# A hybrid decoder layer: all matmul tiles at one offset within 2 KB, an eleventh home for expert pieces

## The chip, the core and the metric

The kernel runs on one core of a Trainium2 chip. The metric is device time in microseconds (us), from the launch of the program on the core to its end; less is better. The engines have short names in the profile: PE (TensorE, matmuls), PEld (its loads of stationary operands), DVE (VectorE), ACT (ScalarE), POOL (GpSimd) and SP (SyncE, which here only issues transfers).

## What is computed

One decoder layer on 256 tokens of width 2048, in float32. Cut to what matters:

```python
h = rms_norm(x, attn_norm_g)
u, q, k, v, gate_ssm, gate_att = split(h @ w_in)          # w_in: 2048 x 8192
y_ssm = s5_mixer(u, ...)                                   # scan over 256 steps, gelu, z * sigmoid(z @ w_glu)
y_att = stick_breaking_attention(rms(q), rms(k), v)        # 8 heads of 128
merged = sigmoid(gate_ssm) * (y_ssm @ w_branch_ssm) + sigmoid(gate_att) * (y_att @ w_branch_att)
x = x + merged @ w_out
t = rms_norm(x, ffn_norm_g)
# router: best of 4 groups, best 2 of its 8 experts; 32 experts in all
for e in range(32):
    out += combine[:, e] * ((silu(t @ w_gate[e]) * (t @ w_up[e])) @ w_down[e])
x = x + out
```

The weights of one expert are 2048 x 1024 (gate and up) and 512 x 2048 (down) in float32, 12.6 MB; those of all experts are 403 MB.

## The kernel before

**Projections.** The weights of w_in, w_branch_att, w_glu, w_branch_ssm and w_out stream through the core in 200 *subs* of 512 KB: two slices of 128 rows by 512 columns each. For each sub, `dma` loads `raw`, and `split` makes two float32r tiles of it: `wh` (ACT, rounded) and `wl` (DVE, what the rounding left). `mm` of `b_orient` then runs twelve matmuls of 512 columns: `wh` against the activations' `xh` and `xl`, and `wl` against `xh`, for two slices and two halves of the tokens. `wh` and `wl` are the moving operand here, and a 128x128 slice of the activations is the stationary one. The names of the activations change with the block: `xh`, `xl` for w_in, `ya` for w_branch_att, `ys` for w_branch_ssm, `m` (`m0`, `m1`) for w_out. Only w_glu (`a_orient`) is the other way round: `wh` and `wl` are stationary, and `zz` is moving, with 256 columns.

The order is written out in a loop over the subs `i`. At each step it splits sub `i + 2`, loads sub `i + 5`, runs the matmuls of sub `i`, and lets the other work (statistics, scan of the state-space mixer, attention heads) take its turns by a rough count of each engine's load. The subs 0 to 143 are w_in and w_branch_att, 144 to 151 w_glu, 152 to 167 w_branch_ssm, 168 to 199 w_out. Three tiles each of `raw`, `wh` and `wl` go round.

**Homes.** Ten tiles of 16 KB a partition, one to a pool, hold large activations during the projections (`U[0]` to `U[9]`, without 6) and then, all but `U[0]` and `U[5]`, serve as homes for *pieces* of expert weights: 2 MB each, six to an expert, 192 in all. `ring` names the order: 8, 9, 2, 7, 4, 3, 1, and three more pools (`w0` to `w2`) where the projections' small tiles had been. `load_piece` takes the next piece and its home. The first six pieces are loaded in quarters of 512 KB from step 148 of the loop on, one quarter at every second step, behind four loads of `x2`; a seventh is loaded whole near the last step. A home can be loaded as soon as its earlier user is done. All these loads, and those of `raw`, stand in one queue on SP, in program order, so a load that waits holds up those behind it.

**Experts.** For each expert, 32 gathered tokens go through `gate_up` (XY stationary, the piece `ew` moving) and `down`; each piece that has been used frees its home for the next. Home 3 is given up after its second piece, since the result `accv` takes its place.

**Places.** The allocator lays the pools out in order, from byte 0 of each partition: 16 KB of scratch for the descriptors of transfers that POOL issues, 128 bytes of constants, the ten tiles of 16 KB, the small tiles (`cp`, `cq`), and then `wp` with `raw`, `wh` and `wl`, and `hp` with eight tiles of 2 KB (`ya` among them). So all the tiles of the first kind start at 128 within 2 KB, and `raw`, `wh`, `wl` and `ya` at 1824:

| tiles | used as | bytes from a partition's start | within 2 KB |
|---|---|---|---|
| xh, xl, m0, m1, ys | stationary | 16,512 to 131,199 | 128 |
| zz (w_glu) | moving | 147,584 | 128 |
| wh, wl | moving (stationary in w_glu) | 186,144 to 210,719 | 1824 |
| ya | stationary | 210,720 to 227,103 | 1824 |

A slice of `wh` or `wl` (512 floats) is 2 KB, and the stationary slices lie at multiples of 512 bytes from their tile's start.

Of the kernel before, what the change touches and what calls it, by code (L numbers as in the profile page):

```python
# [9 lines left out]
F32 = mybir.dt.float32  # L10
# [7 lines left out]
P = 128  # L18
# [18 lines left out]
X2_AT = 24  # L37
# [5 lines left out]


class Meter:
    """Forwards to an engine and adds up a rough length of what is emitted on it."""

    def __init__(self, eng, load, key):
        self.eng, self.load, self.key = eng, load, key
# [33 lines left out]
def hybrid_block(ctx, tc, A, out):  # L83
    nc = tc.nc
# [3 lines left out]
    pe = Meter(nc.tensor, load, "pe")  # L88
    sp, pool = nc.sync, nc.gpsimd

    U = {i: ctx.enter_context(tc.tile_pool(name=f"u{i}", bufs=1)) for i in range(10) if i != 6}

    def unit(i, shape, dt, name):
        return U[i].tile(shape, dt, name=name, tag="u")

# [5 lines left out]
    cq = wctx.enter_context(tc.tile_pool(name="cq", bufs=1))  # L101
# [9 lines left out]
    def bg_tile(k):  # L111
        return pbg.tile([P, 512], F32, name="bg" + "ab"[k], tag="bg" + "ab"[k])

    # ---------------------------------------------------------------- weight stream
    blocks = []

    def add_block(src, nk, begin, mm, fin):
# [6 lines left out]
    def dma(i):  # L124
        if i >= len(subs):
            return
        src, s = subs[i][:2]
        raw_t[i] = wp.tile([P, 2, 512], F32, name="raw", tag="raw")
        sp.dma_start(raw_t[i], src[:, 2 * s:2 * s + 2, :])

    def split(i):
        if i >= len(subs):
            return
        raw = raw_t.pop(i)
        h = wp.tile([P, 2, 512], F32R, name="wh", tag="wh")
        l = wp.tile([P, 2, 512], F32R, name="wl", tag="wl")
        act.copy(h, raw)
        vec.tensor_tensor(l, raw, h, op=OP.subtract)
        hl_t[i] = (h, l)

    # ---------------------------------------------------------------- first loads
    xh = unit(0, [P, 16, T], F32R, "xh")
    xl = unit(1, [P, 16, T], F32R, "xl")
    xT = unit(4, [P, 16, T], F32, "xT")
    g1 = cq.tile([P, 16], F32, name="g1")
    # projection blocks are declared below; the stream is started once they are known
    small = cq.tile([P, 3, 32], F32, name="lamdt")
    dsk = cq.tile([P, 16], F32, name="dsk")
    qkg = cq.tile([P, 2], F32, name="qkg")
    g2 = cp.tile([P, 16], F32, name="g2")  # L150
# [2 lines left out]

    ident = cp.tile([P, P], F32, name="ident")
    make_identity(nc, ident)
    pool.dma_start(small, A["lamdt"])
    ones = cp.tile([P, P], F32, name="ones")
    pool.memset(ones, 1.0)
    uge = cq.tile([P, P], F32, name="uge")
# [36 lines left out]
        vec.tensor_scalar(t, t, -0.5, 1.5, op0=OP.mult, op1=OP.add)  # L196
        vec.tensor_tensor(y, y, t, op=OP.mult)

    # ---------------------------------------------------------------- blocks of the projections
    rstd = cq.tile([P, 2], F32, name="rstd")  # L200
    rstdp = cq.tile([P, 2], F32, name="rstdp")
    uy = unit(2, [P, 2, 8, T], F32, "uy")
# [209 lines left out]
        for s in range(nk // 2):  # L412
            subs.append((src, s, nk, begin, mm, fin))

    # ---------------------------------------------------------------- start of the stream
    def x_prep(k0):
        for k in range(k0, k0 + 2):
            act.activation(xh[:, k], xT[:, k], AF.Copy, scale=g1[:, k:k + 1])
            vec.scalar_tensor_tensor(xl[:, k], xT[:, k], g1[:, k:k + 1], xh[:, k], op0=OP.mult, op1=OP.subtract)
# [61 lines left out]
        vec.tensor_scalar(qkg[:, 0:1], qkg[:, 0:1], float(P) ** -0.5, None, op0=OP.mult)  # L481
        yield 0.8

    # ---------------------------------------------------------------- state-space mixer
    coef = [cq.tile([P, 2, 2, 16], F32, name=f"coef{h}") for h in range(2)]
    prod = [cq.tile([P, 2, 2, 16], F32, name=f"prod{h}") for h in range(2)]

# [249 lines left out]
            yield 0  # L737
        prog["z"] = True

    # ---------------------------------------------------------------- stick-breaking attention  # L740
    hst = cq.tile([P, 3, 2, 2, 8], F32, name="hst")

    def attention():
# [80 lines left out]
        if len(YA) == 8:  # L824
            prog["att"] = True

    # ---------------------------------------------------------------- expert weight stream
    ring = [U[i] for i in (8, 9, 2, 7, 4, 3, 1)]
    used = [0]
    held = {}  # L830
    ahead = []
# [4 lines left out]
    nextp = [0]  # L836

    def load_piece():
        n = nextp[0]
        if n >= len(pieces):  # L840
            return
        j = n % 10 if n < 20 else (n - 20) % 9
        j += n >= 20 and j > 4
        if used[0] <= held.get(j, -1):
            return
        held[j] = n
        e, i = pieces[n]
        tl = ring[j].tile([P, 4, 1024], F32, name="ew", tag="u")
        src = A["wgu"][e][:, 4 * i:4 * i + 4] if i < 4 else A["wd"][e][:, 4 * i - 16:4 * i - 12]
        if n < 6:  # L850
            for k in range(4):
                ahead.append(lambda k=k: sp.dma_start(tl[:, k], src[:, k]))
        else:
            for c0, cw in (((0, 1024),) if n < len(pieces) - 1 else ((0, LSPLIT), (LSPLIT, 1024 - LSPLIT))):
                sp.dma_start(tl[:, :, c0:c0 + cw], src[:, :, c0:c0 + cw])
        ptile[e, i] = tl
        nextp[0] += 1

    # ---------------------------------------------------------------- main stream
    gens = [init_stats(), attention(), ssm()]  # L860
    next(gens[2])
    pend = []
# [25 lines left out]
    first_out = nsub - 32  # L888
    for i in range(nsub):
        prog["step"] = i  # L890
        src, s, nk, begin, mm, fin = subs[i]
        if i < 6:
            x_prep(2 * i + 4)
        split(i + 2)
        dma(i + 5)
        if s == 0:
            begin()
        h, l = hl_t.pop(i)
        mm(s, h, l)
        run_pend()  # L900
        if s == nk // 2 - 1:
            fin()
        pe0 = load["pe"]
        for g in (gens[:1] if i < HOLD else list(gens)):
            while rest.get(g, 0) <= i:
                if load["pe"] > pe0 + BURST or load["vec"] > load["pe"] + SLACK or load["act"] > load["pe"] + SLACK:
                    break
                c = next(g, None)
                if c is None:
                    gens.remove(g)  # L910
                    break
                if c <= 0:
                    rest[g] = i + 1 - c
        load["vec"] = max(load["vec"], load["pe"] - CREDIT)
        load["act"] = max(load["act"], load["pe"] - CREDIT)
        if i == first_out - X2_AT:
            S["x2"] = unit(5, [P, 2, D], F32, "x2")
            for t in range(2):
                for c in range(2):
                    cs = slice(1024 * c, 1024 * c + 1024)  # L920
                    ahead.append(lambda t=t, cs=cs: sp.dma_start(S["x2"][:, t, cs], A["x"][t][:, cs]))
        if i >= first_out - X2_AT and (i % 2 == 0 or i < first_out - X2_AT + 4):
            if not ahead and nextp[0] < 6:
                load_piece()
            if ahead:
                ahead.pop(0)()
        if i == nsub - 4:
            load_piece()
# [6 lines left out]
    for i in range(3):  # L935
        ring.append(ctx.enter_context(tc.tile_pool(name=f"w{i}", bufs=1, reuse_waits="tile")))

    # ---------------------------------------------------------------- router
    def keep_busy(n):
        ps = acc_tile()  # L940
        for _ in range(n):
# [36 lines left out]
    m1, m2 = R4[:, 2], R4[:, 3]  # L978
# [26 lines left out]
    Go = R32[:, 5].rearrange("p t g e -> p t (g e)")  # L1005

    def gates():
        # gate of the first choice: 1 / ((1 + exp(m2 - m1)) * sum of the group softmax)
        vec.tensor_scalar(w1, dif, 1.0, None, op0=OP.add)
        vec.tensor_tensor(w1, w1, gsum[:, :, None].to_broadcast([P, 2, 4]), op=OP.mult)  # L1010
        vec.reciprocal(w1, w1)
        vec.tensor_tensor(w2_, w1, dif, op=OP.mult)
        vec.tensor_tensor(oh1, oh1, w1[:, :, :, None].to_broadcast([P, 2, 4, 8]), op=OP.mult)
        vec.tensor_tensor(oh2, oh2, w2_[:, :, :, None].to_broadcast([P, 2, 4, 8]), op=OP.mult)
        vec.tensor_tensor(R32[:, 2], oh1, oh2, op=OP.add)
        vec.scalar_tensor_tensor(Go, rank, float(CAP), G, op0=OP.is_ge, op1=OP.mult)

    def overflow():
        # experts with more tokens than slots, as a list of ids behind its length
        ps = bg_tile(1)  # L1020
        for t in range(2):
            pe.matmul(ps[0:32, 0:1], M[:, t], ones[:, 0:1], start=(t == 0), stop=(t == 1))
        vec.tensor_scalar(OV[:, 0:1], ps[0:32, 0:1], float(CAP), None, op0=OP.is_gt)
        vec.tensor_tensor(OV[:, 33:34], OV[:, 0:1], eidx[0:32], op=OP.mult)
        pe.matmul(ps[0:32, 1:2], ult[0:32, 0:32], OV[:, 0:1], start=True, stop=True)
        vec.tensor_copy(OV[:, 34:35], ps[0:32, 1:2])
        vec.tensor_scalar(OV[:, 1:33], iota[0:32], OV[:, 34:35], OV[:, 33:34], op0=OP.is_equal, op1=OP.mult)
        pe.matmul(ps[0:1, 2:35], ones[0:32, 0:1], OV[:, 0:33], start=True, stop=True)
        vec.tensor_copy(oli, ps[0:1, 2:35])
# [2 lines left out]
    XB = XY[:, 0]  # L1032
    Y4 = XY[:, 1].rearrange("p a b -> p (a b)")

    # ---------------------------------------------------------------- experts
    SC = [None, None]

    def gather(q):
# [91 lines left out]
            if q == NE // 4 - 1:  # L1130
                sp.dma_start(out[t][:, c], accv[:, t, c])

    while nextp[0] < 10:
        load_piece()
    for e in range(NE - 2):
        hT = gate_up(e, gather(e // 4) if e % 4 == 0 else iter(()))
# [20 lines left out]
    scatter(q, 2, (1,))  # L1157
    scatter(q, 3)

    # ---------------------------------------------------------------- tokens beyond the slots  # L1160
    accv = S["acc"]
    XO = unit(2, [P, 16, T], F32, "XO")
    WO = [unit(u, [P, 4, 1024], F32, f"WO{u}") for u in (4, 9, 7, 0)]
# [3 lines left out]
    with tc.For_i(0, novr) as it:  # L1167
        er = nc.values_load(oli[0:1, bass.ds(it + 1, 1)], min_val=0, max_val=NE - 1)
        gp = [acc_tile() for _ in range(4)]
        for k4 in range(4):  # L1170
# [8 lines left out]
            for i in range(4):  # L1179
                k = 4 * k4 + i  # L1180
                for t in range(2):
                    for hf in range(2):
                        pe.matmul(gp[2 * t + hf], XO[:, k, P * t:P * t + P], WO[k4][:, i, 512 * hf:512 * hf + 512],
                                  start=(k == 0), stop=(k == 15))
# [12 lines left out]
        for t in range(2):  # L1197
            for n in range(4):
                ps = acc_tile()
                for j in range(4):  # L1200
                    pe.matmul(ps, hOT[:, j, P * t:P * t + P], WO[n // 2][:, j, 512 * (n % 2):512 * (n % 2) + 512],
                              start=(j == 0), stop=(j == 3))
# [57 lines left out]
```

## Time and profile before

| what | value |
|---|---|
| three runs | 1598.7, 1601.5 and 1602.9 us |
| median | 1601.51 us |
| profiled execution | span of 1600.2 us, from the first to the last instruction |
| PE busy | 1284.2 us (80%), mean granted clock 0.924 |
| DVE, ACT, POOL busy | 522.9, 451.0 and 43.7 us |
| moved by DMA | 519 MB, 324 GB/s over the span |

The profile is of one execution. A slice or a stretch shows for each engine how long it was busy in it; PEclk is the granted clock of TensorE, 1.00 being 2.4 GHz; the DMA share is the mean busy share of the 16 DMA engines. Matmuls overlap, so the length of one record is more than the distance between two starts; the distance is what a stream of them costs. In the order of time, neighbouring instructions of one form are merged, with their count behind x.

### The profile page before, as it was taken

How to read it: one execution, taken by the hardware profiler on the slowest of the kernel's cores; microseconds unless marked ns; L12 is line 12 of the kernel's file. 1: busy time of each engine (PE TensorE's matmuls, PEld its weight loads, DVE VectorE, ACT ScalarE, POOL GpSimd, SP SyncE). 2: the span in 40 equal slices, each digit the busy share in tenths (PEclk: the TensorE clock that was granted, in tenths of full speed). 3: DMA queues.
4: the chain of work that ended last, by engine and by line, in shares of the span. 5: the costliest groups of instructions: out<-in, count | busy, mean ns of one | idle time of the engine just before them, and what ended most of it. 6: DMA issues, size and time to landing. Idle time of an engine off the chain costs nothing. (4 is left out here: it accounts for less than half of the span.)

```text
span 1600.2 us, 25136 instructions
## 1 busy us (share of the span) xinstructions
PE 1284.2 (80%) x10654; PEld 862.1 (54%) x10654; DVE 522.9 (33%) x1342; ACT 451.0 (28%) x769; POOL 43.7 (3%) x113
## 2 busy tenths in 40 slices
PE   8899999999999999986756656766656656756696
PEld 7777888888867888842423422423323323323364
DVE  5664877787745754410101101101001001001001
ACT  5455567544434443321111011011111111110101
POOL 8200000000000000000000000000000000000000
PEclk9999999999999999997988978978979978888999
DMA  7554645566644777799999999999999999999995
GB/s 270 174 159 147 195 147 157 159 189 193 186 143 160 261 263 261 297 411 429 427 426 428 425 430 425 428 427 427 428 427 428 426 427 428 427 428 426 427 426 233
DMA packets 64131, 519.01 MB, mean 324 GB/s; under 512 B 7680, under 2 KB 7680, under 8 KB 40208
## 3 DMA queue, kind: packets, MB, share of 16 engines
q1 hardware_dynamic: 63408, 515.22, 81.6%
q10 hardware_dynamic: 576, 2.10, 0.4%
q8 instruction: 86, 1.41, 0.4%
q14 instruction: 29, 0.24, 0.0%
q0 software_dynamic: 32, 0.05, 0.0%
HBM read 515.24 MB, written 2.10 MB: 323 GB/s over the span
## 5 line engine op out<-in xcount | busy, mean ns | idle before, releaser
L77 PE MATMUL acc<-ew,XY 128*32 128x256 f32 x4096 | 303.4, 448 | 170.0 <-DMA ew<-wgu 170.0
L77 PEld LDWEIGHTS acc<-ew,XY 128*32 128x32 f32 x4096 | 140.3, 124 | 317.2 <-DMA ew<-wgu 185.8
L77 DVE TENSOR_TENSOR wl<-raw,wh 128x1024 fp32r<-128x1024 f32 x200 | 244.3, 1225 | 173.3 <-ACT wh L77 168.3
L77 ACT CAST wh<-raw 128x1024 fp32r<-128x1024 f32 x200 | 209.0, 1051 | 198.1 <-PE acc L77 109.6
L77 DVE TENSOR_TENSOR sg<-sg,acc 128x128 f32<-128x128 f32 x32 | 9.2, 288 | 652.4 <-ACT sg L77 652.4
L77 PE MATMUL acc<-ew,hT 128*32 128x256 f32 (+1 forms) x2080 | 152.9, 445 | 76.2 <-DMA ew<-wd 46.1
L77 ACT COPY XY<-acc 32x256 f32<-32x256 f32 (+1 forms) x260 | 93.7, 360 | 220.1 <-PE acc L77 217.6
L77 PEld LDWEIGHTS acc<-ew,hT 128*32 128x32 f32 x2080 | 75.1, 125 | 143.8 <-issue 65.3
L77 PE MATMUL acc<-wh,xh 128*128 128x512 f32 x512 | 147.9, 406 | 3.4 <-ACT wh L77 3.4
L77 PE MATMUL acc<-wl,xh 128*128 128x512 f32 x512 | 144.0, 398 | 1.0 <-DVE wl L77 0.8
L77 PE MATMUL acc<-wh,xl 128*128 128x512 f32 x512 | 144.0, 398 | 0.0
L77 ACT ACTIVATE sg<-acc 128x128 f32<-128x128 f32 x32 | 8.9, 278 | 410.4 <-PE acc L77 410.4
L77 PEld LDWEIGHTS acc<-wl,xh 128*128 128x128 f32 x512 | 97.2, 190 | 25.6 <-DVE wl L77 2.7
L77 PEld LDWEIGHTS acc<-wh,xl 128*128 128x128 f32 x512 | 97.4, 190 | 23.1
L77 PEld LDWEIGHTS acc<-wh,xh 128*128 128x128 f32 x512 | 94.0, 191 | 25.6 <-ACT wh L77 5.6
L77 PE MATMUL acc<-XY,sc 128*128 128x512 f32 x128 | 63.9, 641 | 14.6 <-ACT XY L77 14.5
L77 PE MATMUL bga<-SL,x 128*128 128x128 f32 x512 | 63.5, 280 | 10.3 <-DVE SL L77 10.3
L77 PEld LDWEIGHTS bga<-SL,x 128*128 128x128 f32 x512 | 59.0, 192 | 22.9 <-DVE SL L77 15.9
L77 DVE TENSOR_TENSOR Vs<-Vs,prod 128x32 f32<-128x32 f32 x508 | 68.1, 189 | 0.0
L77 DVE TENSOR_TENSOR accv<-accv,acc 128x512 f32<-128x512 f32 x56 | 38.5, 688 | 86.5 <-PE acc L77 86.5
L77 PE MATMUL acc<-wh,m 128*128 128x512 f32 x256 | 66.4, 399 | 0.0
L77 PEld LDWEIGHTS acc<-wh,m 128*128 128x128 f32 x256 | 47.7, 188 | 11.1
(229 smaller groups left out, 984.6 us busy)
## 6 DMA issues: line engine op xcount, KB each, us to landing
ew<-wgu SPq DMA_DIRECT2D x124, 2048.0 KB, 39.2
ew<-wd SPq DMA_DIRECT2D x61, 2048.0 KB, 39.2
raw<-win SPq DMA_DIRECT2D x128, 512.0 KB, 3.8
raw<-wout SPq DMA_DIRECT2D x32, 512.0 KB, 4.2
raw<-wba SPq DMA_DIRECT2D x16, 512.0 KB, 4.7
raw<-wbs SPq DMA_DIRECT2D x16, 512.0 KB, 5.1
ew<-wgu SPq DMA_DIRECT2D x16, 512.0 KB, 5.6
raw<-wglu SPq DMA_DIRECT2D x8, 512.0 KB, 4.5
```

The lines of the kernel that those rows point to most:

```text
L77: return f(out, *args, **kw)
```

## The change

Four edits, all on places and on the stream of expert pieces:

- the scratch for descriptors shrinks from 16 KB to 1 KB. The one transfer that POOL issued, `lamdt`, moves to ACT's queue;
- the 15 KB and what was unused hold an eleventh large tile, `U[10]`. It has no user during the projections and stands first in `ring`;
- a tile of 352 bytes, `level`, which nothing reads or writes, stands ahead of the small tiles' other contents. With it `wp` starts at 1152 within 2 KB, where the large tiles now start too: 1024 bytes of scratch and 128 of constants;
- seven pieces instead of six are loaded in quarters, and the first four quarters start eight steps sooner.

The rest of the diff takes out comments.

```diff
-    U = {i: ctx.enter_context(tc.tile_pool(name=f"u{i}", bufs=1)) for i in range(10) if i != 6}
+    U = {i: ctx.enter_context(tc.tile_pool(name=f"u{i}", bufs=1)) for i in range(11) if i != 6}
...
     small = cq.tile([P, 3, 32], F32, name="lamdt")
+    cq.tile([P, 88], F32, name="level")
...
-    pool.dma_start(small, A["lamdt"])
+    nc.scalar.dma_start(small, A["lamdt"])
...
-    ring = [U[i] for i in (8, 9, 2, 7, 4, 3, 1)]
+    ring = [U[i] for i in (10, 8, 9, 2, 7, 4, 3, 1)]
...
-        j = n % 10 if n < 20 else (n - 20) % 9
-        j += n >= 20 and j > 4
+        j = n % 11 if n < 22 else (n - 22) % 10
+        j += n >= 22 and j > 5
...
-        if n < 6:
+        if n < 7:
...
-        if i >= first_out - X2_AT and (i % 2 == 0 or i < first_out - X2_AT + 4):
-            if not ahead and nextp[0] < 6:
+        if i >= first_out - X2_AT - 8 and (i % 2 == 0 or 0 <= i - first_out + X2_AT < 4):
+            if not ahead and nextp[0] < 7:
...
-    while nextp[0] < 10:
+    while nextp[0] < 11:
...
-    nc = _bacc.Bacc("TRN2", target_bir_lowering=False, num_devices=1)
+    nc = _bacc.Bacc("TRN2", target_bir_lowering=False, num_devices=1, dynamic_dma_scratch_size=1024)
```

After the change xh, xl, m0, m1, ys, zz, wh, wl and ya all start at 1152 within 2 KB. On PE, DVE and POOL the instructions keep their order (POOL loses the issue of `lamdt`). On SP the rows move at two places.

The first place is the end of w_in's blocks and w_glu (`x` is `x2`, the residual's input, which takes the place of a tile that the state-space mixer uses to the end). Before:

```order
L129 DMA raw<-win 128x1024 x32
L129 DMA raw<-wglu 128x1024 x6
L921 DMA x_4618<-x 128x1024
L129 DMA raw<-wglu 128x1024
L921 DMA x_4618<-x 128x1024
```

After:

```order
L129 DMA raw<-win 128x1024 x30
L853 DMA ew<-wgu 128x1024
L129 DMA raw<-win 128x1024 x2
L853 DMA ew<-wgu 128x1024
L129 DMA raw<-wglu 128x1024 x2
L853 DMA ew<-wgu 128x1024
L129 DMA raw<-wglu 128x1024 x2
L853 DMA ew<-wgu 128x1024
L129 DMA raw<-wglu 128x1024 x2
L922 DMA x_4627<-x 128x1024
L129 DMA raw<-wglu 128x1024
```

Four quarters of the first piece now stand among the last loads of win and those of wglu, ahead of x2.

The second place is the end of w_out, where the loads in quarters end and those of whole pieces (128x4096) begin. Before:

```order
L852 DMA ew<-wd 128x1024
L129 DMA raw<-wout 128x1024 x2
L852 DMA ew<-wd 128x1024
L855 DMA ew<-wgu 128x4096 x4
L855 DMA ew<-wd 128x4096 x2
```

After:

```order
L853 DMA ew<-wgu 128x1024
L129 DMA raw<-wout 128x1024 x2
L853 DMA ew<-wgu 128x1024
L856 DMA ew<-wgu 128x4096 x3
L856 DMA ew<-wd 128x4096 x2
```

The quarters at this place belong to the second expert's first piece now, and three whole pieces of wgu follow where four did.

## Rows read from the trace of the kernel before

**Rows 1.** The page: span; PE's and DMA's busy tenths in 40 slices.
```profile
span 1600.2 us, 25136 instructions
...
PE   8899999999999999986756656766656656756696
...
DMA  7554645566644777799999999999999999999995
```

**Rows 2.** Stretches: from:to, length, busy us (xcount) by engine, PEclk, DMA share, GB/s.
```profile
100.00:332.00 232.00, 232.00 (x1249) 188.63 (x1248) 159.20 (x533) 138.80 (x175) 0.00 (x0) 1.00 0.51 159
332.00:374.90 42.90, 42.90 (x191) 35.51 (x190) 37.48 (x133) 16.48 (x18) 0.00 (x0) 1.00 0.62 193
374.90:464.00 89.10, 89.10 (x382) 71.65 (x381) 67.52 (x267) 37.56 (x39) 0.00 (x0) 1.00 0.60 188
...
502.00:665.00 163.00, 162.76 (x811) 135.36 (x810) 88.32 (x95) 69.78 (x91) 0.00 (x0) 1.00 0.78 267
...
675.00:680.00 5.00, 5.00 (x61) 3.95 (x60) 0.85 (x2) 0.00 (x0) 0.00 (x0) 1.00 0.86 311
1200.00:1400.00 200.00, 131.76 (x1459) 67.23 (x1451) 20.86 (x39) 23.18 (x67) 0.00 (x0) 0.86 1.01 427
```

**Rows 3.** Waits of PE to 700 us: for whom, us in total, times, longest.
```profile
PE bga L77 <- DVE rstd L77: 4.2, 1, 4.2
PE acc L77 <- ACT wh L77: 3.4, 4, 1.5
```

**Rows 4.** Order of time, PE: start us, length us, engine, line, form, xcount.
```profile
342.38 1.98 PE L77 MATMUL acc<-wh,ya 128*128 128x512 f32 x8
...
347.82 1.98 PE L77 MATMUL acc<-wh,ya 128*128 128x512 f32 x8
...
375.02 1.10 PE L77 MATMUL acc<-wh,xh 128*128 128x512 f32 x4
375.96 1.09 PE L77 MATMUL acc<-wh,xl 128*128 128x512 f32 x4
...
405.94 1.10 PE L77 MATMUL acc<-wh,xh 128*128 128x512 f32 x4
...
414.38 1.10 PE L77 MATMUL acc<-wh,xh 128*128 128x512 f32 x4
```

**Rows 5.** Groups by form, xcount | busy, mean ns; and the stretch to 45.6 us, acc's alone.
```profile
L77 PE MATMUL acc<-wh,xh 128*128 128x512 f32 x512 | 147.9, 406 | 3.4 <-ACT wh L77 3.4
...
L77 PE MATMUL acc<-wl,ys 128*128 128x512 f32 x64 | 18.2, 396 | 0.0
...
0.00:45.60 45.60, 35.10 (x150) 28.51 (x151) 0.00 (x0) 0.00 (x0) 0.98 0.77 274
```

**Rows 6.** Order of time, PE, in w_glu.
```profile
509.65 2.08 PE L77 MATMUL acc<-zz,wh 128*128 128x256 f32 x16
...
512.53 2.08 PE L77 MATMUL acc<-zz,wh 128*128 128x256 f32 x16
```

**Rows 7.** A wait of SP's queue; the transfers in quarters: xcount, KB each, us to landing.
```profile
SPq L921 <- PE bga L77: 22.7, 1, 22.7
...
ew<-wgu SPq DMA_DIRECT2D x16, 512.0 KB, 5.6
```

**Rows 8.** Order of time, SP's queue and PE, from the last quarter to the experts.
```profile
654.03 14.81 SPq L855 DMA_DIRECT2D ew<-wgu  x4
...
676.52 1.93 PE L77 MATMUL acc<-ew,XY 128*32 128x256 f32 x32
...
678.51 5.96 SPq L855 DMA_DIRECT2D ew<-wd  x2
```

**Rows 9.** Order of time at the start: POOL's issue of lamdt, ACT, POOL's first use.
```profile
1.48 0.79 POOL L156 DMA_DIRECT2D lamdt<-lamdt  x1
...
4.49 1.28 ACT L77 ACT_TABLE_LOAD   x1 [4.49 <-DMA xT<-xT]
...
6.84 0.33 POOL L533 TENSOR_SCALAR sm<-lamdt 128x32 f32<-128x32 f32 x1
```

## The prediction

> **What bounds the kernel now.** I read the slices of the span first [rows 1], then the stretches [rows 2], then TensorE's waits and its order of time in one stretch. The slices show two stages. In the first, to about 690 us, PE stands at 9 tenths and the DMA engines at 4 to 7; in the second, to the end, the DMA engines stand at 9 and PE at 5 to 7. The stretches give the numbers: from 100 to 464 us and from 502 to 665 us PE is busy all the time at granted clock 1.00 (2.4 GHz) with a DMA share of 0.51 to 0.78; from 1200 to 1400 us the DMA share is 1.01 at 427 GB/s and PE is busy 132 of 200 us. So the projections are bound by PE, the experts by the stream of their weights. The two are joined by homes: the stream can run ahead only into tiles that the projections have given up, and the last three homes come free when the projections end. A shorter projection stage therefore moves the whole expert stage forward, and each expert piece that is already on the chip by then takes its transfer off the second stage.
>
> PE hardly waits in the first stage: its longest waits there are 4.2 us on rstd at 43.96 us and 3.4 us in four waits on wh [rows 3]. What it does all the time is stream 512 columns of wh or wl against a stationary 128x128 slice. **How far apart two such matmuls start** is the number that this change is about. The order of time [rows 4] gives it without a model: with ya as the stationary tile, 24 matmuls start between 342.38 and 347.82, 226.7 ns each. With xh and xl, 36 start between 405.94 and 414.38, 234.4 ns each. The pace changes with the operand and nothing else: right behind the last ya matmul, four on xh take from 375.02 to 375.96, 235 ns each. Same form, same moving tiles, same clock, VectorE as busy (37.5 of 42.9 us beside ya, 67.5 of 89.1 us after it [rows 2]). What differs is the place: wh and wl lie at 1824 within 2 KB, and so does ya, while xh, xl, m and ys lie at 128. 512 columns at 2.4 GHz are 213.3 ns, so both pay something beyond the columns: 13.4 ns and 21.1 ns.
>
> **The change part by part.**
>
> *One offset.* After the change xh, xl, m, ys, zz and wh, wl, ya all lie at 1152. The trace of before has equal offsets only in the ya matmuls, so 226.7 ns is the nearest row, and I take it. The seven forms that now pay 234.4 ns count 512 + 512 + 512 + 256 + 128 + 128 + 64 = 2112 (the first and the last of the seven stand in [rows 5]). Of these about 120 run before 45.6 us (150 matmuls into acc [rows 5] less the 30 warm-up ones of W0), ahead of the wait on rstd, and what they gain is lost in that wait, since rstd comes from ACT and VectorE. 1992 x 7.7 ns = 15.3 us. The bounds: nothing (the offset has no part in it), and the columns alone, 21.1 ns x 1992 + 13.4 ns x 192 (ya) = 44.6 us. I take 15.3, because the ya rows are the same instruction on the same moving tiles.
> The 192 matmuls of wglu have wh stationary and zz moving, at unlike offsets today, and 24 of them take 2.88 us [rows 6]: 120.0 ns, which is 256 columns (106.7 ns) and 13.3 ns, as much beyond the columns as ya pays. I cost their edit at nothing.
>
> [...]
>
> *What lies beside it.* VectorE must deliver wl 3% faster. Beside ya it already does so at the new pace, busy 37.5 of 42.9 us (87%), and PE waits for nothing there. The DMA engines carry a share of 0.78 from 502 to 665 us; 3% more is 0.81. Neither becomes the bound.
>
> *The eleventh home.* A piece is 2 MB (2.097 MB). Its tile has no earlier user, so its four loads of 512 KB, now placed between the last win and the wglu loads on SP's queue, wait for nothing. The loads queued behind them are raw pieces. Four quarters over eight steps of 2.81 us add 2.097 MB / 22.5 us = 93 GB/s to the 188 GB/s of that stretch; 281 GB/s is close to the 267 GB/s that the stretch 502 to 665 us carries with PE busy throughout [rows 2]. So PE hides it. If that cover were gone, each quarter would hold up one raw load by at most 0.524 MB / 427 GB/s = 1.2 us, 4.9 us in all. The 24 quarter loads of before keep their places; each now carries the next piece in order. The transfers of x2, at the same place in the queue as before, wait 22.7 us for PE [rows 7], and the new loads stand ahead of that wait, not behind it.
> What it gives: the second stage has one piece less to move, 2.097 MB / 427 GB/s = 4.9 us. The holes of the crossing stay: the fourth whole piece is issued by 668.8 us, the next goes out at 678.51 [rows 8], when PE has used the first piece, and the DMA share dips to 0.86 from 675 to 680 us [rows 2]. The new home doesn't close that hole; it takes one piece off what comes behind it. Bounds 0 and 4.9 us; I take 4.9, since the stream is at 1.01 from there on.
>
> *The scratch, lamdt, the pad.* lamdt goes from POOL's queue to ACT's. ACT's first work waits for xT until 4.49 us, so the issue lies in idle time; POOL uses lamdt at 6.84 us [rows 9]. One of SP's loads of xT now takes the semaphore that lamdt's landing has to clear first; that may hold it for a microsecond (an estimate: lamdt is issued 1 us sooner than before and used at 6.84 us then), ahead of the rstd wait, where PE stands idle for 4.2 us. I cost these at nothing (bounds -0.8 us, which is POOL's issue, and +1 us). The stages of the experts keep their operands' distances (both sides move by 1024), and they wait for DMA anyway.
>
> **Sum.** The profiled execution spans 1600.2 us; the median of the three runs is 1601.5, 1.3 us above, for what lies around the span and the spread. 1600.2 - 15.3 - 4.9 = 1580.0, and with the same 1.3 us 1581.3.
>
> **The rivals.**
> 1. *The offset means nothing, the home pays.* For it: the wglu matmuls pay no more than ya although their offsets differ, and both have a stationary tile above byte 186,000 of a partition, at 32 within 64 bytes; perhaps that is what makes ya quick, and xh at 1152 (0 within 64, as now) gains nothing. Against it: a wglu matmul is half as long, so what it pays beside a load of weights need not compare, and of the form with 512 columns ya is the only one at equal offsets and the only quick one. 1601.5 - 4.9 = 1596.6, just past 0.3%.
> 2. *Equal offsets cost (the slower side).* If ya is quick because it lies near wh (both between bytes 186,000 and 229,000), and equal offsets bring both reads to the same part of the memory at once, the price by the mirror of the ya rows is +7.7 ns x 1992 = 15.3 us: 1601.5 + 15.3 - 4.9 = 1611.9. It decides from 4.9 ns per matmul (9.7 us, 4.9 of them to eat the home's gain). Against it: the only rows with equal offsets are the quickest of their form.
> 3. *The offset pays, the home doesn't* (the quarters hold up raw loads by as much as they save): 1601.5 - 15.3 = 1586.2.
> 4. *The offset frees the reads wholly*, down to the columns: 1601.5 - 44.6 - 4.9 = 1552. No row of this form comes near it.
>
> **How the numbers follow.** A measurement of this kernel can tell about 0.3% (4.8 us) from no change. Forecast 0.66 at 1581.3, its own spread 1577 to 1586 (a step of 1 ns is 2 us); rival 1 0.19, rival 2 0.05, rival 3 0.05, rival 4 0.05. Rival 1 stands on the edge of 0.3%, so half of it counts as faster: 0.66 + 0.10 + 0.05 + 0.05 = 0.86; same 0.09; slower 0.05. The range leaves out rivals 2 and 4: 1576 to 1597.
>
> **What would show it.** In the order of time of the new kernel, 36 matmuls on xh should take 8.16 us, not 8.44; wglu's 24 should stay near 2.88. The first expert matmul should start about 15 us sooner than 676.52 us [rows 8]. Twenty loads of 512 KB from wgu should stand where 16 did [rows 7], four of them landing before the wait for x2, and the stretch at 427 GB/s should be one piece shorter. The prediction is wrong if the xh pace stays at 234 ns (rival 1), if PE shows new waits on wh or wl, or if the second stage's rate falls below 427 GB/s.

## The result and the profile after

| kernel | median, us | executions | ratio to before, with its 95% interval |
|---|---|---|---|
| before | 1600.62 | 4, from 1598.7 to 1602.87 | |
| after | 1583.58 | 4, from 1582.88 to 1584.44 | 0.9889 [0.9877, 0.9902] |

The changed kernel is faster by 17.0 us (1.1%), with the forecast at 1581.3 and the range from 1576 to 1597. Its profiled execution has a span of 1581.8 us, where before had 1600.2 [rows 1]: 18.4 us less.

The page of after: the span, the busy tenths of PE and of the DMA engines in 40 slices, two groups by form (busy us, mean ns of one | idle time before them), and the transfers of wgu by size.

```profile
span 1581.8 us, 25130 instructions
...
PE   8899999999999999977657657657757657657697
...
DMA  8454655566654877899999999999999999999996
...
L77 PE MATMUL acc<-wh,xh 128*128 128x512 f32 x512 | 145.4, 401 | 3.2 <-ACT wh L77 3.2
...
L77 PE MATMUL acc<-wl,xh 128*128 128x512 f32 x512 | 140.7, 392 | 1.1 <-DVE wl L77 1.0
...
ew<-wgu SPq DMA_DIRECT2D x123, 2048.0 KB, 39.1
...
ew<-wgu SPq DMA_DIRECT2D x20, 512.0 KB, 5.5
```

The two stages are as before, the first bound by PE and the second by DMA. Twenty transfers of 512 KB stand where sixteen did [rows 7]. Two stretches of after, with the columns of [rows 2]:

```profile
332.00:460.00 128.00, 128.00 (x604) 103.98 (x602) 99.30 (x375) 53.05 (x56) 0.00 (x0) 1.00 0.66 210
...
1200.00:1400.00 200.00, 132.30 (x1483) 68.55 (x1475) 20.85 (x39) 24.85 (x72) 0.00 (x0) 0.87 1.01 427
```

PE is busy throughout the first of them at a granted clock of 1.00, VectorE for 99.3 of 128 us, and the stream of the experts still moves 427 GB/s. The order of time on PE in after, on xh (from the first row to the last 36 matmuls start), in w_glu, at the first expert and at the last:

```profile
396.10 1.07 PE L77 MATMUL acc<-wh,xh 128*128 128x512 f32 x4
...
404.26 1.07 PE L77 MATMUL acc<-wh,xh 128*128 128x512 f32 x4
...
500.63 2.08 PE L77 MATMUL acc<-zz,wh 128*128 128x256 f32 x16
...
503.52 2.08 PE L77 MATMUL acc<-zz,wh 128*128 128x256 f32 x16
...
663.53 1.93 PE L77 MATMUL acc<-ew,XY 128*32 128x256 f32 x32
...
1569.31 1.08 PE L77 MATMUL acc<-ew,hT 128*32 128x128 f32 x32
```

36 matmuls on xh take 8.16 us, or 226.7 ns each, the pace that ya had in [rows 4]; w_glu's 24 take 2.89 us against 2.88 [rows 6]. The last row of before that answers to the last one here is this:

```profile
1586.62 1.08 PE L77 MATMUL acc<-ew,hT 128*32 128x128 f32 x32
```

So the 18.4 us fall into three: 13.0 until the first expert matmul (676.52 [rows 8] to 663.53), 4.3 from there to the last expert (910.1 to 905.8) and 1.1 behind it, where the output is stored (13.6 to 12.5).

PE's order up to the experts is the same in both kernels, so the n-th distance between two starts of before can be set beside the n-th of after. That splits the 13.0 us:

| matmuls of 512 columns on the seven forms, after 45.6 us in before | count | ns from start to start, before and after | sum, us |
|---|---|---|---|
| between two others of the kind, up to 260 ns | 1872 | 234.1 and 227.7 | -12.0 |
| first or last beside other work | 101 | 287.7 and 285.8 | -0.2 |
| between two others, over 260 ns (a wait of PE, or the granted clock of 0.50 behind the wait on rstd) | 19 | 450.4 and 450.7 | 0.0 |

These are 12.2 us. The other 0.8 us is already there when the first of these matmuls starts (45.66 us in before, 44.83 in after); that stretch differs from execution to execution, as the last experiments show.

### The profile page after: what moved, and what is told of

The parts are those of the page before. It is cut to its first block, busy times and chain, and to the rows that moved or that the text cites. A ratio compares the mean times of both kernels' runs of the same rounds, so it can differ in the third digit from the quotient of the medians.

```text
span 1581.8 us, 25130 instructions
## 1 busy us (share of the span) xinstructions
PE 1269.7 (80%) x10654; PEld 859.6 (54%) x10654; DVE 523.5 (33%) x1342; ACT 450.8 (28%) x769; POOL 42.9 (3%) x112
## 5 line engine op out<-in xcount | busy, mean ns | idle before, releaser
L77 PE MATMUL acc<-ew,XY 128*32 128x256 f32 x4096 | 310.7, 456 | 171.7 <-DMA ew<-wgu 171.6
L77 PE MATMUL acc<-ew,hT 128*32 128x256 f32 (+1 forms) x2080 | 146.9, 431 | 70.8 <-DMA ew<-wd 39.3
L77 PE MATMUL acc<-wl,xh 128*128 128x512 f32 x512 | 140.7, 392 | 1.1 <-DVE wl L77 1.0
```

The costliest lines, as they stand in the source:

```text
L77: return f(out, *args, **kw)
```

## The experiments

### One part at a time

**offset_only**: before with the pad alone. All matmul tiles then lie at 128 within 2 KB, the homes stay ten, and lamdt and the scratch stay as they were.

```diff
     small = cq.tile([P, 3, 32], F32, name="lamdt")
+    cq.tile([P, 88], F32, name="level")
```

> The kernel before with the 352-byte pad alone: ten homes, 16 KB of scratch, lamdt on POOL. xh, xl, m, ys, zz, wh, wl and ya all start at 128 within 2 KB. Theory (equal offsets let the stream of matmuls run at an even 226.7 ns): 36 matmuls on xh in an undisturbed stretch take 8.16 us, the first expert matmul comes about 12 us sooner than 676.5 us, and the whole is 12 to 13 us shorter than before, about 0.992 of it. Rival (the pace of the changed kernel comes from the smaller scratch, the new addresses or the moved lamdt, not from equality): pace 8.44 us for 36, time as before within 2 us.

Measured: 1590.8 us (11 executions, 1580.0 to 1593.5) against 1601.2, ratio 0.9937 [0.9913, 0.996]. The xh pace is 227 ns. From the first ya matmul to the first expert matmul it takes 338.3 us, as long as after; before takes 345.1. The theory came out, within the width of the interval.

**home_only**: after without the pad. wh lies at 800, xh at 1152.

```diff
     small = cq.tile([P, 3, 32], F32, name="lamdt")
-    cq.tile([P, 88], F32, name="level")
```

> The changed kernel without the 352-byte pad: eleven homes, 1 KB of scratch, lamdt on ACT, but wh and wl at 800 within 2 KB and xh at 1152, so offsets are unequal as before. Theory: xh pace back at 234.4 ns (8.44 us for 36), first expert matmul within 1 us of the kernel before (676.5 us) or 0.8 us sooner if the start gains from lamdt, and the whole 4.3 to 5.5 us shorter than before (0.997). Rival (the home takes nothing off, and the missing 1.5 us of the profiled gain is noise): within 1 us of before.

Measured: 1594.78 us (12 executions, 1585.9 to 1596.9), ratio 0.9964 [0.9944, 0.9985]. The xh pace is 234 ns and the first expert matmul stands at 676.01 us, as before; from there to the last expert it takes 4.4 us less. The theory came out, with a gain 0.9 us above its range and an interval of 3.3 us to either side.

The two parts give 10.4 and 6.4 us, 16.8 together, and the whole change gives 17.0: they add up as far as can be told, since each of the two is known to some 3.5 us either way. offset_only also takes the absolute place out of the question. ya was quick at 1824 in before, and here xh, m and ys are quick at 128, the very place where they were slow in before. Only the distance between the moving and the stationary tile differs. Every execution also holds its own control: the pad moves ya together with wh and wl, so that ya's distance is 0 in all the kernels of this document, and its 190 distances have a mean of 226.8 or 226.9 ns in all thirteen profiles, whatever xh, m and ys do beside it.

### How near must the two places be?

Five kernels are after with another pad, so that wh, wl and ya lie elsewhere and xh, m, ys stay at 1152 within 2 KB. The diff of the first; the others have 72, 56, 104 and 152 in place of 80.

```diff
-    cq.tile([P, 88], F32, name="level")
+    cq.tile([P, 80], F32, name="level")
```

**apart_32** (80 floats): wh at 1120.

> The changed kernel with the pad 32 bytes shorter: wh, wl and ya at 1120, xh at 1152 within 2 KB, 32 bytes apart. Theories A and B both: xh pace 234 ns and about 1596 us, since neither the place within 512 bytes nor that within 64 agrees. Were it 226.7 ns, the condition would be looser still (a multiple of 32), which the 160 bytes within 512 of the kernel before speaks against.

**apart_64** (72 floats): wh at 1088.

> The changed kernel with the pad 64 bytes shorter: wh, wl and ya at 1088, xh and the others at 1152 within 2 KB, 64 bytes apart. Theory A (the offsets must agree within 512 bytes or more): xh pace 234 ns, time about 1596 us. Theory B (what counts is that both start at a multiple of 64 bytes, or agree within 64): xh pace stays 226.7 ns, time about 1583 us.

**apart_128** (56 floats): wh at 1024.

> The kernel after with a pad of 56 floats: wh, wl and ya at 1024 within 2 KB, xh and the other large tiles at 1152, 128 apart. Theory A (the quick pace needs equal places modulo 256): the xh matmuls start 231 to 238 ns apart, the first expert matmul stands near 674 us and the time is about 1594 us. Theory B (modulo 128 is enough): 226.7 ns, first expert matmul near 664, about 1584 us.

**above_64** (104 floats): wh at 1216.

> The changed kernel with the pad 64 bytes longer: wh, wl and ya at 1216, xh at 1152, so the moving tile lies 64 bytes above the stationary one (64 below gave 234 ns on xh, but 116 instead of 120 ns on w_glu, where the roles are swapped). Theory (any unequal offset breaks the even pace): xh pace 234 ns, about 1594 us. Rival (the sign matters, as w_glu hints): xh pace under 226.7 ns, 222 to 223, and w_glu back at 120 or more; about 1576 us.

**above_256** (152 floats): wh at 1408.

> The changed kernel with the pad 256 bytes longer: wh, wl and ya at 1408, xh at 1152, half of 512 apart. Theory (the period is 512 bytes, since ya's slices at 0, 512, 1024 and 1536 from wh all ran at 226.7): xh pace 231 to 238 ns, about 1594 us. Rival (the period is 256 or 128): xh pace 226.7 ns, about 1584 us.

Measured, one execution each, with before, home_only and after beside them, whose times are medians. The pace is the mean of the 369 distances up to 260 ns between two neighbouring matmuls of w_out (m stationary), that of w_glu the mean of 187.

| kernel | wh minus xh, modulo 256 | w_out, ns | w_glu, ns | first expert matmul, us | time, us |
|---|---|---|---|---|---|
| after | 0 | 227.1 | 121.0 | 663.53 | 1583.58 |
| above_256 | 0 (256 apart) | 227.1 | 121.1 | 664.78 | 1585.74 |
| above_64 | 64 | 229.0 | 114.7 | 667.05 | 1587.34 |
| apart_128 | 128 | 232.3 | 119.8 | 673.60 | 1593.16 |
| home_only | 160 | 234.2 | 121.1 | 676.01 | 1594.78 |
| before | 160 | 234.2 | 121.1 | 676.52 | 1600.62 |
| apart_64 | 192 | 233.3 | 116.7 | 674.10 | 1594.28 |
| apart_32 | 224 | 233.2 | 118.4 | 672.95 | 1593.66 |

The same 36 matmuls on xh in the order of time, first above_64:

```profile
395.80 1.08 PE L77 MATMUL acc<-wh,xh 128*128 128x512 f32 x4
...
404.04 1.08 PE L77 MATMUL acc<-wh,xh 128*128 128x512 f32 x4
```

then apart_128:

```profile
396.40 1.10 PE L77 MATMUL acc<-wh,xh 128*128 128x512 f32 x4
...
404.76 1.10 PE L77 MATMUL acc<-wh,xh 128*128 128x512 f32 x4
```

and home_only:

```profile
396.98 1.10 PE L77 MATMUL acc<-wh,xh 128*128 128x512 f32 x4
...
405.41 1.10 PE L77 MATMUL acc<-wh,xh 128*128 128x512 f32 x4
```

8.24, 8.36 and 8.43 us, where after has 8.16. So 256 apart is as good as equal, and 128 apart is not: as far as this one pair shows it, the pace goes by the distance modulo 256, not modulo 2 KB as the change puts it. The theories by which 64, 32 and 128 bytes short are slow came out (apart_64, apart_32, apart_128); the period of 512 that above_256 was to show did not, and above_64 lies between its two, at 229.0 ns where one had 234 and the other 222 to 223. It isn't a matter of quick or slow either. It grows from 0 over 64 and 128 to 160, and 32 or 64 short of the next 256 is still slow. In w_glu, where wh is stationary and zz moves, equal places are not the best: a quarter of 256 to either side takes 114.7 or 116.7 ns against 121.0. Why the distance acts in this way, no run here shows.

### Is the pace found again after other work?

**interrupt**: after with one transpose, which nothing reads, ahead of each of the 24 subs 120 to 143.

```diff
+        if 120 <= i < 144:
+            pe.transpose(bg_tile(1)[:, 0:P], ident, ident)
```

> The changed kernel with one 128-column transpose of the identity (not used) ahead of each of the 24 subs 120 to 143, where PE's stream is otherwise undisturbed. In the changed kernel's trace the matmuls 2 to 10 behind another kind of work start 228 to 233 ns apart, and from the 11th on 226.7. Theory (the even pace has to be found again after each interruption): within each sub of this stretch the starts 3 and 4 are near 233 ns and the last ones near 227, the mean about 229.5; the whole 24 x (0.11 + 0.1 + 0.03) = 5 to 6 us longer than the changed kernel. Rival (the slower starts come from what other engines do beside such work): all starts from the second on at 226.7, the whole 4 to 5 us longer.

Measured: 1587.12 us, first expert matmul at 667.83 us (after: 663.53). The order of time on PE, one sub between two transposes (bgb):

```profile
397.00 0.27 PE L77 MATMUL bgb<-ident 128*128 128x128 f32 x1
397.02 1.18 PE L77 MATMUL acc<-wh,xh 128*128 128x512 f32 x4
398.04 1.07 PE L77 MATMUL acc<-wh,xl 128*128 128x512 f32 x4
398.95 1.08 PE L77 MATMUL acc<-wl,xh 128*128 128x512 f32 x4
399.86 0.27 PE L77 MATMUL bgb<-ident 128*128 128x128 f32 x1
```

The first four take 1.02 us, the next four 0.91. The mean over 21 subs: 318.9 ns from the first to the second (the change of work is in it), then 234.4, 232.3 and 231.0, then 226.8 and about 227 up to the next transpose. So the quick pace is not there at once; it is found again within a few matmuls, at a loss of some 17 ns. The theory came out in kind, and the rival (226.7 ns from the second on) falls; the whole is 3.5 us longer, not 5 to 6. With the transpose itself (25.8 ns) and the change of work (92 ns) that is 135 ns, or 3.2 us for 24 of them, of the 4.3 us by which the first expert matmul is later. In after itself, behind the statistics, the scan and the attention heads, it takes longer: from the second matmul behind other work to the eleventh, the nine distances are 229.7, 232.9, 232.8, 228.1, 230.7, 231.3, 227.6, 229.1 and 228.4 ns (about 50 cases each), and the later ones 226.8. Whether this longer way is the same thing, or comes from what the other engines do beside such work, was not tried; in before these nine are uneven too, from 231.2 to 237.2 ns.

### What moves the start

The times of one kernel gather at two places. In the 22 executions of before that stand beside offset_only and home_only, it took 1591.4 to 1592.2 us four times and 1599.4 to 1604.1 otherwise; offset_only took 1580.0 and 1580.4 twice of 11 and 1587.9 to 1593.5 otherwise. The profiled execution of offset_only (span 1578.7 us) is one of its two shorter ones. Around rstd, the order of time of after (columns as in [rows 4]; in brackets the idle time before, and what ended it):

```profile
34.77 3.52 POOL L562 MEMSET BBD<- 128x4096 f32 x1
...
36.12 5.63 DVE L77 TENSOR_SCALAR rtmp<-rtmp 128x2 f32<-128x2 f32 x1
...
38.22 3.51 POOL L563 MEMSET CBD<- 128x4096 f32 x1
...
43.13 0.98 PE L77 MATMUL bga<-rstd,perm 128*128 128x1 f32 x4 [5.23 <-DVE rstd L77]
```

and of offset_only:

```profile
35.47 0.17 DVE L77 TENSOR_SCALAR rtmp<-rtmp 128x2 f32<-128x2 f32 x1
...
37.07 0.56 PE L77 MATMUL bga<-rstd,perm 128*128 128x1 f32 x4
...
38.13 3.53 POOL L562 MEMSET BBD<- 128x4096 f32 x1
```

A VectorE instruction on two elements takes 5.63 us in after and 0.17 in offset_only, and in after it ends (41.75) with POOL's second memset (41.73). Where POOL's memsets come later than it, it isn't held. The same holds in before, where it starts between the two memsets' starts and ends with the second (37.98 + 4.60 = 42.58 against 39.05 + 3.51 = 42.56 us):

```profile
35.59 3.52 POOL L561 MEMSET BBD<- 128x4096 f32 x1
...
37.98 4.60 DVE L77 TENSOR_SCALAR rtmp<-rtmp 128x2 f32<-128x2 f32 x1
...
39.05 3.51 POOL L562 MEMSET CBD<- 128x4096 f32 x1
```

Of the thirteen profiles nine have the instruction start beside the memsets, and in each it ends 0.02 or 0.03 us behind the second; in the other four it takes 0.17 us. In after and before the hold lasts from within the first memset to the end of the second. By what means a memset holds it, no run shows. What the wait costs beyond its 5.2 us is seen in the stretches of after behind it (columns as in [rows 2]):

```profile
43.00:46.00 3.00, 2.87 (x11) 2.71 (x12) 3.00 (x5) 1.82 (x2) 0.00 (x0) 0.50 0.27 56
46.00:50.00 4.00, 4.00 (x14) 3.18 (x13) 1.61 (x4) 1.35 (x2) 0.00 (x0) 0.67 0.85 303
```

After the idle time PE goes on at a granted clock of 0.50 to 48 us; it is 0.70 from 48 to 49 and 1.00 from 49 to 50, and 0.67 is the mean from 46 to 50. The order of time has four matmuls at each clock, 2.05 and 1.09 us long:

```profile
44.83 2.05 PE L77 MATMUL acc<-wh,xh 128*128 128x512 f32 x4
...
49.43 1.09 PE L77 MATMUL acc<-wh,xh 128*128 128x512 f32 x4
```

That the hold is also what parts the shorter from the longer executions of one program is an inference: no program has a profile of both.

**memset_sooner**: after with the two memsets issued some 16 us sooner, behind the first exponential of the state-space mixer's setup on POOL.

```diff
         dt = dexp(ldt, new())
+        BBD = unit(9, [P, 2, 32, 2, 32], F32, "BBD")
+        CBD = unit(5, [P, 4, 32, 32], F32, "CBD")
+        pool.memset(BBD.rearrange("p a b t c -> p (a b t c)"), 0.0)
+        pool.memset(CBD.rearrange("p a b c -> p (a b c)"), 0.0)
         mag = dexp(mul(lr, dt), new())
...
         tt(den, den, t, OP.add)
-        BBD = unit(9, [P, 2, 32, 2, 32], F32, "BBD")
-        CBD = unit(5, [P, 4, 32, 32], F32, "CBD")
-        pool.memset(BBD.rearrange("p a b t c -> p (a b t c)"), 0.0)
-        pool.memset(CBD.rearrange("p a b c -> p (a b c)"), 0.0)
```

> The changed kernel with POOL's two 3.5 us memsets (BBD, CBD) moved some 20 us forward, between the two exponentials, so that they no longer stand beside VectorE's work on rstd. In the changed kernel's trace the tensor_scalar on rtmp (2 columns) takes 5.63 us from 36.12 while the memsets run, PE then waits 5.2 us for rstd and runs its next 12 matmuls at about half pace; in the run with the pad alone the same instruction took 0.17 us, ahead of the memsets, and rstd came at 37.07. Theory (VectorE's instruction is held until both memsets are done): rstd's matmul near 37 us in every run, no slow mode, the whole 7 to 10 us shorter than the changed kernel's 1583.6, about 1575. Rival (the 5.6 us is a wait for ACT or for a transfer, and the early runs are early for another reason): rstd stays near 43 us, time within 2 us of 1583.6.

Measured: 1577.31 us (6 executions, 1573.4 to 1577.9), ratio 0.9852 [0.9826, 0.9878]. It beats both kernels, after by 6.3 us, a little less than the 7 to 10 us expected. The profiled execution is the shortest of the six. Its order of time:

```profile
21.98 3.52 POOL L554 MEMSET CBD<- 128x4096 f32 x1
...
36.07 0.17 DVE L77 TENSOR_SCALAR rtmp<-rtmp 128x2 f32<-128x2 f32 x1
...
37.68 0.56 PE L77 MATMUL bga<-rstd,perm 128*128 128x1 f32 x4
```

and the stretches behind it:

```profile
40.00:43.00 3.00, 3.00 (x14) 2.48 (x14) 1.24 (x2) 0.68 (x1) 2.52 (x6) 1.00 1.00 349
43.00:46.00 3.00, 3.00 (x14) 2.48 (x14) 0.92 (x3) 1.15 (x2) 1.53 (x5) 1.00 1.01 410
```

In it the hold, PE's wait and the low clock are all gone, so the theory came out and the rival (rstd stays near 43 us) falls.

**before_memset**: before with the same four lines moved and nothing else.

> The kernel before with only POOL's two memsets issued sooner. Theory A (the memsets hold VectorE's tensor_scalar in the chain to rstd in most executions, whatever the kernel): rstd is used near 37.7 us instead of 43.96, the executions near 1591 us that now and then appear become the rule, and the median is 1591 to 1596 us. Theory B (only the new kernel's start gains from it): 1599 to 1602 us.

Measured: 1594.45 us (6 executions, 1591.5 to 1597.6) against 1601.46, ratio 0.9957 [0.9945, 0.9969]; the tensor_scalar takes 0.17 us and the rstd matmul starts at 38.95 us (before: 43.96). Theory A came out in the median and in rstd's time, but not in all: the executions near 1591 us did not become the rule, only one of the six lies there.

**memset_no_pad**: memset_sooner without the pad, so eleven homes and unequal places.

```diff
-    cq.tile([P, 88], F32, name="level")
```

> The kernel after with POOL's two memsets issued sooner and without the pad: eleven homes, wh at 800 and xh at 1152 within 2 KB. It measures the equal offsets alone, by its distance from the same kernel with the pad (1577.3 us), both with a start in which VectorE isn't held. Theory A (equal offsets are worth about 12 us by the matched matmuls, whatever the start): 1587 to 1591 us, xh pace about 235 ns. Theory B (what the three comparisons with and without the pad showed was partly the start's two modes): the distance is 6 us or less, 1583 us or less.

Measured: 1587.26 us (5 executions, 1586.0 to 1589.3) against 1601.46, ratio 0.9915 [0.9902, 0.9927], xh pace 234 ns. Theory A came out.

These three start without the hold, and give the parts so: 7.2 us for the home with the scratch and lamdt (1594.45 to 1587.26), 10.0 us for the equal places (1587.26 to 1577.31), and 7.0 us for the memsets. The matched distances of memset_no_pad and memset_sooner give 12.1 us for 1855 matmuls, as before and after do; the 10.0 is a difference of two medians whose executions spread over 3.3 and 4.5 us, each beside executions of before of its own (medians 1601.46 and 1601.57). memset_sooner's times still gather at two places (two at 1573.4 and 1573.7, four from 1577.3 to 1577.9); only one of the first two was profiled, so what parts them stays open.

## Why the prediction was right, and where its sizes were off

**The bound and the way to the end.** Right. A projection stage that is 13.0 us shorter starts the experts 13.0 us sooner, and nothing of it is given back: the second stage keeps 427 GB/s.

**One offset: right in kind, 12.2 us in place of 15.3.** The step that failed is the multiplication. The ya rows [rows 4] gave 226.7 ns, and the new pace of xh is just that, but the prediction gave the gain of 7.7 ns to all 1992 matmuls. ya's block is a single run of matmuls with nothing between them; the others are cut some 50 times by other work. Four parts make up the missing 3.1 us: 120 matmuls at a cut, at a wait or at the low clock gain 0.2 us where the sum had 0.9, which leaves 0.7; the nine distances behind each of some 50 cuts, 438 in all, went from 233.9 to 230.1 ns on average and gained 3.8 ns instead of 7.7 (1.7 us); 48 matmuls between 45.6 and 62 us kept 233 ns, 0.4 us; and the steady pace of the other 1386 gained 7.5 ns instead of 7.7, 0.3 us. The 48 belong to u's two blocks, whose stationary slices take every second token, so that neighbouring columns are not neighbours in memory; that this is why equal places don't help them was not tried alone. Their pace does go by the distance, but otherwise: their distances up to 245 ns (165 to 173 of them) have a mean of 233.2 ns at 160 (before) and 233.3 at 0 (after), but 231.6 at 128 (apart_128) and 230.2 at 192 (apart_64). The 109 matmuls of these blocks before 45.6 us also kept 233 ns, so the reason why the prediction left them out (their gain is lost in the wait on rstd) was not needed.

One reading beside it was loose: the prediction called VectorE as busy beside xh as beside ya [rows 2]. It was busy for 76% of the one stretch and 87% of the other, and the quick pace stood in the busier one, so this doesn't weaken the argument.

**The eleventh home: 4.3 us in place of 4.9 in the second stage.** (The large tiles themselves are nine in before and ten in after; seven and eight of them are homes, and the three pools `w0` to `w2` make ten and eleven.) Measured to the start of the very last matmul of the experts, the stage takes 910.2 to 912.0 us in the three kernels with ten homes and 906.5 to 907.7 in the ten with eleven. PE hides the extra quarters, as forecast: its longest waits before 700 us, and that on wl, are these.

```profile
PE bga L77 <- DVE rstd L77: 5.2, 1, 5.2
PE acc L77 <- ACT wh L77: 3.2, 3, 1.7
PE acc L77 <- ACT XY L77: 3.2, 2, 1.6
...
PE acc L77 <- DVE wl L77: 1.0, 3, 0.4
```

They answer to [rows 3], with no new wait on wh or wl. The waits on XY belong to the experts, one in each; after has two of them before 700 us and before has one, because its experts start sooner. The medians give the home 6.4 to 7.2 us, more than the stage. Part of that lies behind the last expert: from the start of its last matmul to the end of the span it takes 12.5 to 12.7 us in the three kernels with ten homes and 9.7 to 11.7 in the ten with eleven. Whether the home, the smaller scratch or lamdt's new queue does that was not tried apart; the prediction had no term for it.

**The scratch, lamdt and the pad: nothing, as forecast.** rstd is used 0.8 us sooner in after, which is less than the start varies by between executions.

**w_glu: nothing, as forecast,** but not for the reason given. The prediction took 13.3 ns beyond the columns as a sign that unequal places cost a matmul of 256 columns nothing. The table shows that they matter there too (114.7 to 121.1 ns): 0 and 160 only happen to cost the same, so this part was right by luck.

**The rivals.** The first (the places mean nothing) falls with offset_only and the table: the pace goes from 227.1 to 234.2 ns over six distances. The second (equal places cost) falls with the same rows: xh is quick at 128, far from wh. The third (the home doesn't pay) falls with home_only, and with memset_no_pad set beside before_memset. The fourth (down to the columns) falls with the pace: 226.7 ns is the lowest steady pace of this form that any kernel reached, 13.4 ns above the 213.3 ns that the prediction took for the columns alone. The rows bear out the 2.4 GHz behind that figure, by an estimate: ya's 226.7 ns for 512 columns [rows 4] less w_glu's 120.0 for 256 [rows 6] is 106.7 ns for 256 columns, or 2.4 columns a ns, though the two forms differ in more than their columns.

**The wait on rstd.** The prediction read it in [rows 3] as a wait for ACT and VectorE and used it as a cover. VectorE was itself held by POOL's memsets (4.60 us for the tensor_scalar in before, 0.17 in before_memset), which the waits don't say; the length of one instruction in the order of time does. Nothing in the forecast hung on it, but it was worth 7 us and was open to anyone who asked why a two-element instruction takes 4.6 us.

The sum for the profiled execution was 20.2 us and came out at 18.4: 12.2 of 15.3 and 4.3 of 4.9, and 0.8 and 1.1 us at the start and at the end that it didn't have. That the forecast came within 2.3 us is luck in part: its two terms were 3.7 us too high, and half of that was made up by what it had put at nothing.

## What to carry to other kernels

Where long matmuls (512 columns here) follow one another with weights loaded for each, try the moving and the stationary tile at the same place modulo 256 bytes of a partition: here w_out's took 227.1 ns each at 0 and 234.2 at 160. For another form try several places: with 256 columns (114.7 ns at 64, 121.0 at 0), or with every second column of the stationary tile (230.2 ns at 192, 233.3 at 0), another distance was best.

The pace to expect is that of an uninterrupted run, less what each cut by other work costs (135 ns for a single transpose here, 17 of them until the pace is found again). A price read from one block holds for blocks that are built alike, so count the cuts before multiplying. When an engine waits for another, look at how long the other's last instruction took before calling it slow: one of 0.17 us took 5.63 here.

## What the runs showed of the hardware

- The distance between two matmuls of 512 float32r columns with new weights each depends on where the moving tile lies against the stationary one: in w_out 227.1, 229.0, 232.3, 234.2, 233.3 and 233.2 ns at 0, 64, 128, 160, 192 and 224 bytes modulo 256. That it repeats after 256 rests on one pair (227.1 ns at 0 and at 256 apart). Why, no run shows.
- The quick pace is found again after other work only over some matmuls: four behind a single transpose (234.4, 232.3, 231.0, then 226.8 ns; shown with nothing else changed), about ten behind the kernel's other work (227.6 to 232.9 ns, then 226.8; seen, its cause not tried).
- Two memsets on POOL (3.5 us each) held a VectorE tensor_scalar of two elements for 5.63 us in after; with the memsets sooner it took 0.17. PE, idle for 5.2 us because of it, went on at a granted clock of 0.50, and was back at 1.00 from 49 us (to 62 us at least). With the memsets issued sooner, before is 7.0 us shorter and after 6.3. That the executions of one program differ by 8 us and more because the two meet or not is inferred.
